# Down products of four blocks as seven-product quads, and gate/up quads that gather in three PSUM banks

## The chip, the cores and the metric

The kernel runs on one core of one Trainium2 chip. The metric is the time on the device, in microseconds (us). The engines are TensorE (PE), which multiplies; VectorE (DVE), ScalarE (ACT) and GpSimd (POOL), which work on tiles in SBUF and PSUM; and SyncE (SP), from whose queue nearly all DMAs are issued.

## The reference

One inference step of a backbone of two layers over 640 tokens (512 latent tokens and 128 context tokens) of 1024 channels. Each layer is a SwiGLU, a mixer, and a second SwiGLU, each behind an RMS norm with adaLN scale and shift, and each added to the residual stream x by a gate:

```
def swiglu(h, w_gate, w_up, w_down):
    return (jax.nn.silu(h @ w_gate) * (h @ w_up)) @ w_down

x = x + 0.5 * mod[:, 2][:, None, :] * swiglu(hh, ffn1_gate[l], ffn1_up[l], ffn1_down[l])
x = x + mod[:, 5][:, None, :] * y                 # y: the mixer's output
x = x + 0.5 * mod[:, 8][:, None, :] * swiglu(hh, ffn2_gate[l], ffn2_up[l], ffn2_down[l])
```

The inner width of a SwiGLU is 2816. The mixer of layer 0 is attention beside a gated linear recurrence, that of layer 1 a Fourier transform with a linear map. The change touches the four SwiGLUs alone.

## The kernel before

**Tiles.** Channels lie on the 128 partitions: 1024 channels are 8 chunks, the inner width is 22 chunks, called f. The tokens are held as two halves h = 0 and 1 of 320 columns each. The residual stream x stays in SBUF (`x_85` and `x_86` in the listings).

**Products.** Every product runs in fp32r as three passes, high × high, high × low and low × high (`mm3`, matmul at L282). So every weight and every right factor is split: ACT copies the high part (L176 for weights, `whi`; L171 for others), and DVE subtracts it from the value for the low part (L181, `wlo`; L172). Weights arrive by DMA in `st` buffers of 128 × 1024 (six in a SwiGLU), and their split parts take one of five slots; a quad's factor S1 has a slot of 512 columns of its own.

**Gate and up (`quad`).** For a chunk f from 2 on, the gate and up weights times the two token halves are a 2 × 2 problem (unit by half of the channels, half of the channels by half of the tokens). It takes seven products of 12 matmuls by Strassen and Winograd, 84 in place of 96:

M1 = A11 B11, M2 = A12 B21, M3 = S4 B22, M4 = A22 T4, M5 = S1 T1, M6 = S2 T2, M7 = S3 T3.

The right factors (B, T) come from the normed input and are made once for a SwiGLU. The left factors are made for each chunk by six steps (L214 to L249): a splits A11 and A12 as one part of 1024 columns; b and c make the sums S1, S3, S2 and S4 in four POOL operations of 512 columns (L226, L227, L231, L232; S1 into the one buffer `sums`); d splits S1 (`s`); e splits S3 beside A22, f splits S2 beside S4. The products run in the order M1, M5, M7, M6, M2, M3, M4, each in a PSUM bank of its own out of six; ACT copies M1, M5 and M7 to SBUF (L826), and DVE and POOL sum (L825). The result g of each half is then split (L171, L172).

**Down.** The 22 chunks go in blocks (`BLK`): six of three f and one of four. A block's down product takes each of the 8 output chunks and both token halves in a plain product over the block's f, 9 matmuls for three f (`down`), and DVE adds gate times the result to x straight from PSUM (`x_update`, L381; half 1 in pieces of 192 and 128 columns, since its tokens have two conditions). The last block (`down_last`) is interleaved with the next norm. A block's down product follows the quad of the next block's first chunk.

**Order.** The order on each engine is that of the program. `prep` emits weight steps from one list, one after each product, up to four items ahead, when its buffers are free; a low part is emitted with the step after its high part (`split_later`, `flush`). Fills (`fill`) are slabs of adaLN products between quads; the last SwiGLU has none there.

## Time and profile before

| | |
|---|---|
| Median of 3 runs | 2306.37 us (2303.54 to 2308.12) |
| Span of the profiled execution | 2305.0 us |
| PE busy | 2224.0 us, 96% |
| DVE busy | 1554.8 us, 67% |
| ACT busy | 990.7 us, 43% |
| POOL busy | 954.9 us, 41% |
| Granted TensorE clock | 0.992 |
| Instructions | 39901 |

The span is the time from the first to the last instruction of one profiled execution, which has no separate time of its own; the median is of other executions. Rows of the trace give an instruction's line, its engine, and `out<-in` by the program's names without buffer numbers. A row of a timeline has the start, the length, and in brackets the idle time before it with what ended it. A PE row of 0.31 us is the length of one matmul in the pipeline, and the next one begins before it ends; the time that a matmul takes up is the step from one start to the next.

### The profile page before, as it was taken

The numbers are of one execution on the slowest core, as the hardware profiler recorded it, in microseconds if no ns is written. First come the engines' busy times: TensorE is split into PE (matmuls) and PEld (weight loads), VectorE is DVE, ScalarE is ACT, GpSimd is POOL, SyncE is SP. The second block draws the span as 40 slices with busy tenths as digits, with TensorE's granted clock in tenths as the row PEclk, the third lists the DMA queues.
The fourth block names the chain that finished last, engine by engine and source line by source line (L and its number), as shares of the span: only waits on it lengthen the run. The fifth ranks groups of instructions, "written<-read, shape, count | busy, mean of one in ns | idle before, by whom it ended". The sixth has DMA issues, their size and how long they took to land.

```text
span 2305.0 us, 39901 instructions
## 1 busy us (share of the span) xinstructions
PE 2224.0 (96%) x15534; PEld 2110.0 (92%) x15534; DVE 1554.8 (67%) x2871; ACT 990.7 (43%) x1780; POOL 954.9 (41%) x856
## 2 busy tenths in 40 slices
PE   7999999999998899999999999999999989999999
PEld 5889999999994788999999889999999979999999
DVE  6676677666865368666666786666667786666665
ACT  4433333347855435333333453333335553333332
POOL 2444444440023235444444454444443645444441
PEclk9999999999999999999999999999999999999999
DMA  7333333321228424333322243332332322222221
GB/s 278 113 111 105 105 107 107 115 74 56 73 71 267 131 83 137 110 101 110 106 91 97 75 155 120 110 97 96 103 117 62 128 85 83 83 83 83 83 89 57
DMA packets 75316, 245.44 MB, mean 106 GB/s; under 512 B 8756, under 2 KB 12996, under 8 KB 75128
## 3 DMA queue, kind: packets, MB, share of 16 engines
q1 hardware_dynamic: 74168, 241.28, 31.7%
q8 instruction: 123, 2.02, 0.4%
q10 hardware_dynamic: 864, 1.38, 0.2%
q14 instruction: 65, 0.53, 0.1%
q0 software_dynamic: 96, 0.22, 0.0%
HBM read 239.71 MB, written 3.15 MB: 105 GB/s over the span
## 4 chain that ended last, share of the span: by engine, by line
PE 79%; DVE 13%; ACT 4%; issue 2%; POOL 2%; DMA 1%; ACTq 0%; DVEq 0%; SPq 0%; POOLq 0%
PE q L282 40%; PE pd L282 26%; PE pj L282 5%; DVE wlo L181 2%; PE ada L327 2%; DVE tl L172 1%; PE pg L282 1%; PE gt L1014 1%; PE pos L1549 1%; DVE x L381 1%; PE S L1262 1%; DVE y L473 1%; DVE sx L1268 1%; PE PT L1288 1%; DMA st<-w_ada 1%
## 5 line engine op out<-in xcount | busy, mean ns | idle before, releaser
L181 DVE TENSOR_TENSOR wlo<-st,whi 128x1024 fp32r<-128x1024 f32 (+2 forms) x401 | 498.4, 1254 | 11.1 <-ACT whi L176 10.2
L176 ACT ACTIVATE whi<-st 128x1024 fp32r<-128x1024 f32 (+2 forms) x405 | 401.2, 992 | 233.0 <-POOL st L232 139.3
L282 PE MATMUL pd<-g,whi 128*128 128x320 f32 x1536 | 347.0, 310 | 4.3 <-DVE u L825 2.3
L381 DVE SCALAR_TENSOR_TENSOR x<-pd,mods,x 128x128 f32<-128x128 f32 (+2 forms) x696 | 265.0, 433 | 111.7 <-PE pd L282 111.2
L282 PE MATMUL q<-hh,wlo 128*128 128x320 f32 x960 | 296.9, 309 | 5.3 <-DVE wlo L181 5.3
L282 PE MATMUL q<-hh,whi 128*128 128x320 f32 x960 | 300.7, 313 | 1.0 <-DVE u L825 1.0
L282 PE MATMUL q<-th,whi 128*128 128x320 f32 x960 | 297.3, 310 | 3.0 <-DVE sg L825 3.0
L282 PE MATMUL q<-tl,whi 128*128 128x320 f32 x960 | 296.6, 309 | 0.7 <-POOL tl L172 0.7
L282 PE MATMUL q<-th,wlo 128*128 128x320 f32 x960 | 296.6, 309 | 0.0
L282 PE MATMUL q<-hl,whi 128*128 128x320 f32 x960 | 296.3, 309 | 0.0
L231 POOL TENSOR_TENSOR st<-sums,st 128x512 f32<-128x512 f32 x80 | 118.0, 1474 | 396.9 <-DVE wlo L181 359.5
L825 POOL TENSOR_TENSOR u<-u,u 128x320 f32<-128x320 f32 x80 | 106.5, 1331 | 401.0 <-DVE u L825 401.0
L282 PEld LDWEIGHTS pd<-g,whi 128*128 128x128 f32 x1536 | 256.8, 188 | 8.9 <-DVE x L381 3.1
L282 PE MATMUL pd<-hh,whi 128*128 128x320 f32 x768 | 238.4, 310 | 0.0
L282 PE MATMUL pd<-hl,whi 128*128 128x320 f32 x768 | 237.9, 310 | 0.0
L282 PE MATMUL pd<-g,wlo 128*128 128x320 f32 x768 | 237.7, 310 | 0.0
L282 PE MATMUL pd<-hh,wlo 128*128 128x320 f32 x768 | 236.8, 308 | 0.0
L826 ACT ACTIVATE sg<-sg 128x320 f32<-128x320 f32 x160 | 75.4, 471 | 284.5 <-DVE sg L825 284.5
L282 PEld LDWEIGHTS q<-hh,whi 128*128 128x128 f32 x960 | 180.2, 188 | 16.8 <-issue 8.6
L282 PEld LDWEIGHTS q<-th,whi 128*128 128x128 f32 x960 | 180.3, 188 | 6.6 <-issue 4.7
L282 PEld LDWEIGHTS q<-hh,wlo 128*128 128x128 f32 x960 | 180.2, 188 | 6.4 <-DVE wlo L181 6.4
L282 PEld LDWEIGHTS q<-tl,whi 128*128 128x128 f32 x960 | 180.4, 188 | 1.5 <-POOL tl L172 1.5
(327 smaller groups left out, 5016.0 us busy)
## 6 DMA issues: line engine op xcount, KB each, us to landing
st<-w_ada SPq DMA_DIRECT2D x144, 512.0 KB, 4.6
st<-ffn_gate SPq DMA_DIRECT2D x88, 512.0 KB, 3.6
st<-ffn_up SPq DMA_DIRECT2D x88, 512.0 KB, 3.7
st<-ffn_down SPq DMA_DIRECT2D x96, 384.0 KB, 3.1
st<-w_in SPq DMA_DIRECT2D x20, 512.0 KB, 3.5
st<-ffn_down SPq DMA_DIRECT2D x16, 512.0 KB, 3.5
st<-w_out_ab SPq DMA_DIRECT2D x8, 512.0 KB, 3.5
st<-w_out_c SPq DMA_DIRECT2D x8, 512.0 KB, 3.5
```

Source lines behind the costliest of these rows:

```text
L172: (eng or self.nc.vector).tensor_tensor(out=lo, in0=src, in1=hi.bitcast(F32), op=ALU.subtract)
L176: self.nc.scalar.activation(out=hi, in_=src, func=AF.Copy)
L181: self.low.tensor_tensor(out=lo, in0=src, in1=hi.bitcast(F32), op=ALU.subtract)
L231: self.nc.gpsimd.tensor_tensor(out=s[:, 0:512], in0=it.s1, in1=s[:, 0:512], op=ALU.subtract)
L282: self.nc.tensor.matmul(out, lhsT=l, rhs=r, start=first and j == 0, stop=last and j == len(ops) - 1)
L327: nc.tensor.matmul(self.ada_ps[32 * j:32 * j + 32, 0:256], lhsT=self.s_sb[:, k, :], rhs=t[:, 256 * j:256 * j + 256], start=k == 0, stop=k ...
L381: self.nc.vector.scalar_tensor_tensor(out=self.x[h][c][:, sl], in0=ps[:, sl], scalar=gate[:, c, r:r + 1], in1=self.x[h][c][:, sl], op0=ALU ...
L473: nc.vector.tensor_tensor(out=y, in0=self.x[h][c], in1=r, op=ALU.mult)
L825: tt = lambda e, o, a, b, op=ALU.add: e.tensor_tensor(out=o, in0=a, in1=b, op=op)
L826: cp = lambda o, p, fn=AF.Copy: nc.scalar.activation(out=o, in_=p, func=fn)
L1014: nc.tensor.matmul(g[:, s, 0:322], lhsT=wt[:, d, j, :], rhs=xc[:, 322 * s:322 * s + 322], start=True, stop=True)
L1262: nc.tensor.matmul(o, lhsT=q, rhs=k, start=True, stop=True)
```

## The change

In each SwiGLU the blocks become four of four f, one of two and one of four. In the first four blocks the down product is done by `down_quad`, twice for a block, once for each four output chunks. It is again a 2 × 2 problem: two output chunks by two f-chunks on the left, two f-chunks by two token halves on the right, for two pairs of outputs q and two pairs of f at once. Each of the seven products is 12 matmuls (two banks q, two pairs of f, three passes), so a down quad has 84 where the plain form has 96, and a block 168 where it has 192. The last six f keep plain products.

The right factors are now made of g. `g_even` and `g_odd` make them for a pair of f (B11, T1; B22, B21, T3, T2, T4), with high parts on ACT (L744 of the changed kernel), low parts on DVE (L747) and subtractions on POOL (L758); `step` advances each by one stage after every product. The result of the last quad before a down product is held back (`g_held`) and goes into its factors only after the two down quads.

A gate/up quad's products run in a new order and gather in three banks: a takes A11, then S2, S1 and S4 on top; b takes S3, then A22; c takes A12. Between them ACT copies the bank to SBUF (L1022): m1, g1 (from b), g0, u5. A product that adds to a bank waits until ACT has copied the sum so far. The steps of the weights are a, b, c, e, f, d. A down quad does the same with pairs of banks (copies at L939), and adds to x in twelve updates of 320 columns, six of which read the copies instead of PSUM (L388); the plain form has eight, all from PSUM.

Also changed: the tags `u3` and `c22` have three buffers each; the heads of the SwiGLUs finish the T factors earlier (`t_end` at (6, 1, 1) instead of (6, 3, 1)); two small parameter loads are issued from ACT's queue instead of POOL's, and the scratch for dynamic DMA is 1024; the down weights are laid out to suit.

```diff
-BLK = (3,) * 6 + (4,)
+BLK = (4,) * 4 + (2, 4)
+NS = 4
...
+GN = ("B11", "B21", "B22", "T1", "T2", "T3", "T4")
+PLAIN = {16: (0, ("B11", "T1")), 17: (0, ("B21", "B22")), 18: (0, ("T2", "T3")), 19: (1, ("B11", "B21")),
+         20: (0, ("B11", "T1")), 21: (0, ("B21", "B22"))}
...
-        s = [(self.quad_a, 1), (self.quad_b, 0), (self.quad_c, 0), (self.quad_d, 2), (self.quad_e, 1), (self.quad_f, 1)]
+        s = [(self.quad_a, 1), (self.quad_b, 0), (self.quad_c, 0), (self.quad_e, 1), (self.quad_f, 1), (self.quad_d, 2)]
         if first:
-            s = s[:3] + s[5:] + s[3:5]
+            s = s[:3] + [s[4], s[5], s[3]]
...
-            w = 2 * nb * P
-            for c in range(0, KD, 2):
-                self.add_w(dn[off:off + P * w].rearrange("(p w) -> p w", p=P), w, ph)
+            w = 1024 if bi < NS else 2 * nb * P
+            part = lambda: dn[off:off + P * w].rearrange("(p w) -> p w", p=P)
+            for c in range(4):
+                if bi < NS and c % 2:
+                    self.add_quad(a0, part(), ph, False)
+                elif bi < NS:
+                    a0 = part()
+                else:
+                    self.add_w(part(), w, ph)
                 off += P * w
...
+    def g_even(self, G, b11, b12):
+        self.hi(G["B11"], b11)
+        yield 1
+        self.lo(G["B11"], b11)
+        yield 1
+        self.sub(b11, b12, b11)
+        yield 1
+        self.hi(G["T1"], b11)
+        yield 1
+        self.lo(G["T1"], b11)
+    def g_odd(self, G, t1, b12, b21, b22):
+        self.hi(G["B22"], b22)
+        self.sub(b12, b22, b12)
+        yield 1
+        self.hi(G["B21"], b21)
+        self.lo(G["B22"], b22)
+        self.sub(t1, b22, t1)
+        yield 1
+        self.lo(G["B21"], b21)
+        self.hi(G["T3"], b12)
+        yield 1
+        self.hi(G["T2"], t1)
+        self.lo(G["T3"], b12)
+        self.sub(b21, b21, t1)
+        yield 1
+        self.lo(G["T2"], t1)
+        self.hi(G["T4"], b21)
+        yield 1
+        self.lo(G["T4"], b21)
...
+    def g_put(self, f, g0, g1, wait=False):
+        if wait:
+            self.g_held = f, g0, g1
+        elif f >= 4 * NS:
+            self.g_jobs.append(self.g_plain(f, g0, g1))
+        elif f % 2 == 0:
+            self.g_last = g0, g1
+            self.g_jobs.append(self.g_even(self.G[f // 2 % 2], g0, g1))
+        else:
+            self.g_jobs.append(self.g_odd(self.G[f // 2 % 2], *self.g_last, g0, g1))
...
-                self.quad(f, qfills.pop(0))
+                self.quad(f, qfills.pop(0), wait=bi < NS and f == end - 1)
                 next(mid, None)
                 f += 1
             if bi == 0:
                 self.ada_end()
             fs = range(sum(BLK[:bi]), sum(BLK[:bi + 1]))
-            if bi == len(BLK) - 1:
+            self.g_end()
+            if bi < NS:
+                for d in range(2):
+                    self.down_quad(d, gate)
+                self.g_put(*self.g_held)
+            elif bi == len(BLK) - 1:
...
+        def mm(p, name, x, first=True, last=False, free=None):
+            for q in pq:
+                self.mm3(p[q], self.need(it, name), (2 * q, 2 * q + 1), [G[x] for G in self.G], first, last, True)
+            if free == "S1":
+                self.s1_free.append(it.slot.pop("S1"))
+            elif free:
+                self.free_slot(it, free)
+        def snap(p, *tags):
+            ts = [self.temp(tags[q % len(tags)]) for q in pq]
+            for t, b in zip(ts, p):
+                nc.scalar.activation(out=t, in_=b, func=AF.Copy)
+            return ts
+        def add(h, i, v):
+            for q in pq:
+                self.x_update(h, 4 * d + 2 * q + i, v[q], gate)
+        a = bank()
+        mm(a, "A11", "B11")
+        m1 = snap(a, "acc0", "acc1")
+        self.step()
+        b = bank()
+        mm(b, "S3", "T3")
+        m7 = snap(b, "c22")
+        self.step()
+        mm(a, "S2", "T2", False)
+        u2 = snap(a, "u3")
+        self.step()
+        c = bank()
+        mm(c, "A12", "B21", last=True, free="A1")
+        add(0, 0, c)
+        self.step()
+        mm(a, "S1", "T1", False, free="S1")
+        u5 = snap(a, "sq")
+        for q in pq:
+            nc.gpsimd.tensor_tensor(out=m7[q], in0=m7[q], in1=u5[q], op=ALU.add)
+        add(0, 0, m1)
+        self.step()
+        mm(b, "A22", "T4", False, True, "S3")
+        add(0, 1, b)
+        self.step()
+        mm(a, "S4", "B22", False, True, "S24")
+        add(1, 0, a)
+        self.step()
+        add(0, 1, u2)
+        add(1, 1, m7)
+    def temp(self, tag):
+        bufs = {"acc0": 1, "acc1": 1, "sq": 2}.get(tag)
+        if bufs:
+            return self.t2.tile([P, HT], F32, tag=tag, name="tmp", bufs=bufs)
+        return self.t3.tile([P, HT], F32, tag=tag, name=f"t{tag}", bufs=3)
+    def step(self):
+        self.prep(self.n_use + 4, 1)
+        self.g_step()
...
+        if chain:
+            it = self.item()
+            a = mm("A11", None, False)
+            m1 = snap(a, "acc0")
+            step()
+            b = mm("S3", None, False)
+            g1 = snap(b, "c22")
+            step()
+            mm("S2", a, False)
+            g0 = snap(a, "u3")
+            step()
+            self.fill(fills // 2)
+            c = mm("A12")
+            sg0, sg1 = sgs()
+            tt(nc.vector, sg0, c, m1)
+            step()
+            mm("S1", a, False)
+            u5 = snap(a, "sq")
+            act(sg0, sg0, AF.Silu)
+            tt(nc.gpsimd, g1, g1, u5)
+            step()
+            mm("A22", b)
+            tt(nc.vector, g0, b, g0)
+            tt(nc.vector, g0, g0, sg0, ALU.mult)
+            step()
+            mm("S4", a)
+            act(sg1, a, AF.Silu)
+            self.ada_end()
+            step()
+            tt(nc.vector, g1, g1, sg1, ALU.mult)
```

The first place is a gate/up quad that follows one of odd f, on ACT, in the last SwiGLU. Before, a quad's row of ACT has its copies of M1 (`m_20481`), M5 (`m_20498`) and M7 (`u_20499`), the high parts of weights (`whi`, `s`) and the two SiLUs.

```order
L826 ACTIVATE m_20481<-q 128x320
L826 ACTIVATE m_20498<-q 128x320
L176 ACTIVATE s_18906<-sums 128x512
L826 ACTIVATE u_20499<-q 128x320
L176 ACTIVATE whi_73<-st_18904 128x1024
L826 ACTIVATE sg<-sg 128x320
L176 ACTIVATE whi_75<-st_18905 128x1024
L826 ACTIVATE sg<-sg 128x320
L171 ACTIVATE g_18910<-c_20501 128x320
```

After, at the end of quad 7 and the start of quad 8: the copies are m1 (`tmp`), g1 (`tc_20490`) and g0 (`tu_20508`), and between them stand high parts of right factors (L744; `hh_91` is that of T3, from `tc_20234`).

```order
L183 ACTIVATE s_18990<-sums 128x512
L183 ACTIVATE whi_73<-st_66 128x1024
L1022 ACTIVATE sg<-q 128x320
L744 ACTIVATE g1B_19010<-tc_20363 128x320
L1022 ACTIVATE tmp<-q 128x320
L183 ACTIVATE whi_67<-st_64 128x1024
L744 ACTIVATE g1B_19008<-tu_20380 128x320
L1022 ACTIVATE tc_20490<-q 128x320
L744 ACTIVATE hh_91<-tc_20234 128x320
L1022 ACTIVATE tu_20508<-q 128x320
L744 ACTIVATE hh_89<-tu_20252 128x320
```

The high part of T3 now stands ahead of the copy of g0, for which the quad's S1 product waits.

On POOL, in a quad before, the four sums of the next weight split are followed by the three sums of the quad's results.

```order
L226 TENSOR_TENSOR sums<-st_18903 128x512
L227 TENSOR_TENSOR st_18903<-st_64,st_18903 128x512
L231 TENSOR_TENSOR st_64<-sums,st_64 128x512
L232 TENSOR_TENSOR st_64<-st_64 128x512
L825 TENSOR_TENSOR u_22855<-u_22855,u_22856 128x320
L825 TENSOR_TENSOR u_22856<-u_22856,m_22854 128x320
L825 TENSOR_TENSOR c_22857<-u_22855,m_22854 128x320
```

After, at the same place as on ACT above, one sum of results (L1021) of quad 7 comes first, then the four sums of the split, then three subtractions (L758), of which the first makes T3 (`tc_20234`).

```order
L1021 TENSOR_TENSOR tc_20363<-tc_20363,tmp 128x320
L233 TENSOR_TENSOR sums<-st_64 128x512
L234 TENSOR_TENSOR st_64<-st_66,st_64 128x512
L238 TENSOR_TENSOR st_66<-sums,st_66 128x512
L239 TENSOR_TENSOR st_66<-st_66 128x512
L758 TENSOR_TENSOR tc_20234<-tc_20363,tc_20234 128x320
L758 TENSOR_TENSOR tu_20252<-tc_20363,tu_20252 128x320
L758 TENSOR_TENSOR tu_20380<-tu_20380,tu_20252 128x320
L1021 TENSOR_TENSOR tc_20490<-tc_20490,tmp 128x320
```

T3 is made behind the four sums of the split, and the first of these writes `sums`, which DVE's low part of quad 7's S1 reads.

The other place is a down product, on DVE. Before, the updates of x (`x_85` half 0, `x_86` half 1) read PSUM (`pd`) and stand between low parts of weights.

```order
L181 TENSOR_TENSOR wlo_76<-st_64,whi_75 128x768
L381 SCALAR_TENSOR_TENSOR x_85<-pd,mods,x_85 128x320
L381 SCALAR_TENSOR_TENSOR x_86<-pd,mods,x_86 128x192
L381 SCALAR_TENSOR_TENSOR x_86<-pd,mods,x_86 128x128
L381 SCALAR_TENSOR_TENSOR x_85<-pd,mods,x_85 128x320
L381 SCALAR_TENSOR_TENSOR x_86<-pd,mods,x_86 128x192
L381 SCALAR_TENSOR_TENSOR x_86<-pd,mods,x_86 128x128
L181 TENSOR_TENSOR wlo_74<-st_18904,whi_73 128x1024
L181 TENSOR_TENSOR s_18907<-sums,s_18906 128x512
```

After, at the end of the first down quad of a block: four updates from PSUM, a low part, then six updates that read the copies u2 (`tu`) and m7 (`tc`).

```order
L388 SCALAR_TENSOR_TENSOR x_86<-pd,mods,x_86 128x192
L388 SCALAR_TENSOR_TENSOR x_86<-pd,mods,x_86 128x128
L388 SCALAR_TENSOR_TENSOR x_86<-pd,mods,x_86 128x192
L388 SCALAR_TENSOR_TENSOR x_86<-pd,mods,x_86 128x128
L188 TENSOR_TENSOR wlo_68<-st_18989,whi_67 128x1024
L388 SCALAR_TENSOR_TENSOR x_85<-tu_20639,mods,x_85 128x320
L388 SCALAR_TENSOR_TENSOR x_85<-tu_20640,mods,x_85 128x320
L388 SCALAR_TENSOR_TENSOR x_86<-tc_20621,mods,x_86 128x192
L388 SCALAR_TENSOR_TENSOR x_86<-tc_20621,mods,x_86 128x128
L388 SCALAR_TENSOR_TENSOR x_86<-tc_20622,mods,x_86 128x192
L388 SCALAR_TENSOR_TENSOR x_86<-tc_20622,mods,x_86 128x128
```

The updates from m7 now come last, and they free the `c22` buffers into which ACT copies the next quad's product S3.

More of the change, by code (lines that the diff above doesn't have):

```diff
@@ L273, in done, with mm3 @@
         self.prep(self.n_use + self.LS, most)
-    def mm3(self, out, w, ks, xs, first=True, last=True):
+    def mm3(self, out, w, ks, xs, first=True, last=True, skip=False):
         ops = []
@@ L715, in gpart, with g_step, g_end, hi @@
     def gpart(self, f, h):
-        return self.g[f % 4][2 * h:2 * h + 2]
-    def g_split(self, f, h, gg):
-        self.split(*self.gpart(f, h), gg)
+        k, n = PLAIN[f]
+        return self.G[k][n[h]]
+    def g_step(self):
+        self.g_jobs = [g for g in self.g_jobs if next(g, None)]
+    def g_end(self):
+        while self.g_jobs:
+            self.g_step()
+    def hi(self, t, src):
+        self.nc.scalar.activation(out=t[0], in_=src, func=AF.Copy)
+    def lo(self, t, src):
+        self.nc.vector.tensor_tensor(out=t[1], in0=src, in1=t[0].bitcast(F32), op=ALU.subtract)
@@ new lines, in g_plain, with sub @@
+    def g_plain(self, f, g0, g1):
+        two = [(self.gpart(f, h), g) for h, g in enumerate((g0, g1))]
+        for t, g in two:
+            self.hi(t, g)
+        yield 1
+        for t, g in two:
+            self.lo(t, g)
+    def sub(self, o, a, b):
+        self.nc.gpsimd.tensor_tensor(out=o, in0=a, in1=b, op=ALU.subtract)
+    def g_even(self, G, b11, b12):
[8 more added lines that the diff above has]
+        self.lo(G["T1"], b11)
@@ L790, in ffn_body, with down_quad @@
                     self.done()
+    def down_quad(self, d, gate):
+        nc = self.nc
+        it = self.item()
+        pq = range(2)
+        bank = lambda: [self.bank("pd")[:, 0:HT] for _ in pq]
+        def mm(p, name, x, first=True, last=False, free=None):
[49 more added lines that the diff above has]
+        self.prep(self.n_use + 4, 1)
+        self.g_step()
     def down(self, p, w, j, h, fs, now):
@@ L818, in down_last, with quad, mm @@
                 self.done()
-    def quad(self, f, fills, begin=False):
+    def quad(self, f, fills, begin=False, wait=False):
         nc = self.nc
         tt = lambda e, o, a, b, op=ALU.add: e.tensor_tensor(out=o, in0=a, in1=b, op=op)
-        cp = lambda o, p, fn=AF.Copy: nc.scalar.activation(out=o, in_=p, func=fn)
-        t3 = lambda n, bufs=2: self.t3.tile([P, HT], F32, tag=n, name=n, bufs=bufs)
+        act = lambda o, p, fn=AF.Copy: nc.scalar.activation(out=o, in_=p, func=fn)
         h, T = self.h, self.T
-        step = lambda: self.prep(self.n_use + 4, 1)
-        def mm(name, xs, free=None):
-            p = self.bank("q")[:, 0:HT]
-            self.mm3(p, self.need(it, name), range(4), xs)
+        step = self.step
+        XS = {"A11": h[0][:4], "A12": h[0][4:], "S4": h[1][4:], "A22": T[3], "S1": T[0], "S2": T[1], "S3": T[2]}
+        chain = f > 2
+        SLOT = {"A12": "A1", "S4" if chain else "S2": "S24", "A22": "S3", "S1": "S1"}
+        def mm(name, p=None, last=True):
+            first = p is None
+            if first:
+                p = self.bank("q")[:, 0:HT]
+            self.mm3(p, self.need(it, name), range(4), XS[name], first, last, chain)
+            free = SLOT.get(name)
             if free == "S1":
@@ L885, in quad, with snap @@
-        tt(nc.vector, u3, u3, sg0, ALU.mult)
-        self.g_split(f, 0, u3)
+        def snap(p, tag):
+            t = self.temp(tag)
+            act(t, p)
+            return t
+        sgs = lambda: [self.t2.tile([P, HT], F32, tag="y", name="sg", bufs=3) for _ in range(2)]
+        if chain:
+            it = self.item()
+            a = mm("A11", None, False)
[26 more added lines that the diff above has]
+            tt(nc.vector, g1, g1, sg1, ALU.mult)
+        else:
+            if not self.begun:
+                it = self.item()
+                m1 = snap(mm("A11"), "acc0")
+                step()
+                c = None
+            else:
+                it, m1, c = self.begun
+            if begin:
+                self.begun = it, m1, mm("A12")
+                return
+            if c is None:
+                c = mm("A12")
+                step()
+            e = mm("S4")
+            step()
+            m5 = snap(mm("S1"), "sq")
+            step()
+            g0 = snap(mm("S3"), "u3")
+            step()
+            self.fill(fills // 2)
+            u2 = self.temp("sq")
+            g1 = self.temp("c22")
+            tt(nc.vector, u2, mm("S2"), m1)
+            tt(nc.gpsimd, g0, g0, u2)
+            tt(nc.gpsimd, u2, u2, m5)
+            tt(nc.gpsimd, g1, g0, m5)
+            step()
+            sg0, sg1 = sgs()
+            tt(nc.vector, sg0, c, m1)
+            act(sg0, sg0, AF.Silu)
+            step()
+            tt(nc.vector, sg1, e, u2)
+            act(sg1, sg1, AF.Silu)
+            tt(nc.vector, g1, g1, sg1, ALU.mult)
+            step()
+            tt(nc.vector, g0, mm("A22"), g0)
+            self.ada_end()
+            tt(nc.vector, g0, g0, sg0, ALU.mult)
@@ L887, in quad @@
+        self.g_put(f, g0, g1, wait)
         step()
```

117 lines of the change are left out of this document (61 added, 56 removed).

## The prediction

> **What bounds the kernel now.** I read the page's head, then the granted clock, then the chain that ended last, then a table by stage, the waits and the timelines. The head shows a TensorE (PE) that is busy almost throughout, and the clock is nearly full, so it is not the throttle that sets the time.
>
> ```profile
> span 2305.0 us, 39901 instructions
> PE 2224.0 (96%) x15534; PEld 2110.0 (92%) x15534; DVE 1554.8 (67%) x2871; ACT 990.7 (43%) x1780; POOL 954.9 (41%) x856
> core 0: 2305.0 us, clock 0.992
> ```
>
> The profiled span of 2305.0 us lies 1.4 below the median of 2306.37, so sums made in the trace carry over to the median as they are. The chain (start, length, what, count) is PE from product to product. Its rows from the last SwiGLU are three gate/up quads (252 matmuls), one down block (144), and three quads; the rows of an earlier one show quads with one fill (an adaLN slab, 8 narrow matmuls) between.
>
> ```profile
> 1473.07 0.57 PE ada L327 x8
> 1473.64 12.52 PE q L282 x84
> ...
> 1945.59 36.98 PE q L282 x252
> 1982.56 21.13 PE pd L282 x144
> 2003.69 36.96 PE q L282 x252
> ```
>
> Hence 21.13/144 = 0.1467 us for a matmul of 320 columns, 1.76 us for a product of twelve, 12.32 us for a quad of 84, and 0.57 for a fill. The table by stage (window, length, then busy time and count of PE, PEld, DVE, ACT, POOL, then clock, DMA share, GB/s) says that PE never stops in the steady state, while the others have room; the waits there (total, times, longest) are on the side of those others.
>
> ```profile
> 1945.00:2275.00 330.00, 330.00 (x2251) 330.00 (x2251) 214.96 (x354) 129.88 (x216) 149.32 (x120) 1.00 0.24 77
> POOL st L231 <- DVE wlo L181: 88.9, 17, 8.4
> ACT whi L176 <- POOL st L232: 28.5, 11, 5.4
> ```
>
> So taking matmuls away shortens the time, as long as the steps that feed PE keep up. Whether they do is the question, and the timelines of DVE and POOL give the prices (start, length, instruction):
>
> ```profile
> 2021.04 1.22 DVE L181 TENSOR_TENSOR wlo<-st,whi 128x1024 fp32r<-128x1024 f32 x1
> 2022.17 0.68 DVE L181 TENSOR_TENSOR s<-sums,s 128x512 fp32r<-128x512 f32 x1
> 2023.50 1.58 DVE L181 TENSOR_TENSOR wlo<-st,whi 128x1024 fp32r<-128x1024 f32 x1
> 2022.42 1.58 POOL L231 TENSOR_TENSOR st<-sums,st 128x512 f32<-128x512 f32 x1 [4.75 <-DVE wlo L181]
> 2024.08 2.16 POOL L232 TENSOR_TENSOR st<-st 128x512 f32<-128x512 f32 x1
> 2026.20 0.87 POOL L825 TENSOR_TENSOR u<-u,u 128x320 f32<-128x320 f32 x1
> ```
>
> The low part that starts at 2023.50 ends at 2025.08, 1.07 after POOL's first sum ended at 2024.00; POOL's second ends at 2026.24, 1.16 after that. They run one after the other: each holds the other off for its whole length. The holds are so 1.07 us for a low part of 1024 columns and 1.16 for a POOL sum of 512. A lone instruction reads 0.15 longer (1.22 against 1.07), so by the rows I take 0.53 for s, 0.73 for a POOL sum of 320, and 0.35 for a DVE operation of 320 that reads two SBUF tiles (0.49 lone). Where DVE reads PSUM and SBUF, there is no such hold: four updates take 0.41 each beside two POOL sums at their lone length.
>
> ```profile
> 2059.40 1.65 DVE L381 SCALAR_TENSOR_TENSOR x<-pd,mods,x 128x320 f32<-128x320 f32 x4
> 2059.63 1.29 POOL L231 TENSOR_TENSOR st<-sums,st 128x512 f32<-128x512 f32 x1 [3.19 <-DVE wlo L181]
> 2061.00 1.30 POOL L232 TENSOR_TENSOR st<-st 128x512 f32<-128x512 f32 x1
> ```
>
> **What is removed.** In each of four SwiGLUs, four blocks of four f-chunks go from 192 to 2 × 84 = 168 matmuls, 24 fewer each: 16 × 24 = 384, which is also the difference of the two programs' PE rows. All were on the chain: 384 × 0.1467 = **−56.3 us**. The last six f-chunks of a SwiGLU keep plain down products.
>
> **What is added and moved.** Per block, two weight splits with four POOL sums, three low parts and s, in place of four plain low parts; right factors of g (7 high parts on ACT, 7 low parts on DVE, 4 POOL subtractions for a pair of f); and, of twelve updates of x in a down quad, six that read SBUF copies instead of PSUM. In holds, a split is 4 × 1.16 + 3 × 1.07 + 0.53 = 8.38, six of them 50.3; the four gate/up quads add 4 × (0.73 + 2 × 0.35) = 5.7; the two pairs' factors 2 × (4 × 0.73 + 7 × 0.35) = 10.7; the down quads 2 × (2 × 0.73 + 6 × 0.35) = 7.1. That is 73.8 us in a block in which PE has 504 × 0.1467 = 73.9, or 76.2 with four fills. DVE and POOL together are thus as full as PE, and any place where one waits in order for the other shows on PE. Two families of places do, by the order of instructions.
>
> *B: the gate/up quad after one of odd f (quads 4, 6, 8, … 16 of a SwiGLU, 28 in all).* S1 is now its fifth product, into a bank that ACT must first have copied out (the copy of g0). On ACT, the high part of T3 stands ahead of that copy; T3 is a POOL subtraction queued behind the four sums of the next weight split; the first of these waits for DVE's low part of S1 (one sums buffer), and that stands behind the previous quad's last two operations on g0. Durations of ACT and the delay from PE to DVE come from these rows (groups: busy, mean ns; the matmul that closes a product issues at 2010.42, the slot after it ends at 2010.57, and DVE starts at 2010.76):
>
> ```profile
> L171 ACT ACTIVATE hh<-u 128x320 fp32r<-128x320 f32 x40 | 18.9, 472 | 76.6 <-DVE u L825 76.6
> L826 ACT ACTIVATE m<-q 128x320 f32<-128x320 f32 x160 | 63.2, 429 | 177.5 <-PE q L282 177.5
> L176 ACT ACTIVATE whi<-st 128x1024 fp32r<-128x1024 f32 x300 | 315.3, 1053 | 227.0 <-POOL st L232 139.3 <-PE pd L282 71.8 <-PE yp L1588 6.2
> 2010.42 0.31 PE L282 MATMUL q<-th,wlo 128*128 128x320 f32 x1
> 2010.76 0.49 DVE L825 TENSOR_TENSOR u<-q,m 128x320 f32<-128x320 f32 x1 [1.84 <-PE q L282]
> ```
>
> From the end of A22: 0.19 + two operations on g0 0.82 + s 0.6 + four sums 4.64 + T3 0.73 + its high part 0.5 + the copy 0.5 = 8.0. Five products pass meanwhile (S4, A11, S3, S2, A12): 8.8. So it is hidden if nothing of DVE's falls between. But two low parts of 1024 and three operations of 320 stand there (2.14 + 1.05 = 3.2), and each takes its turn with a POOL sum: 11.2, a wait of 2.4. I take 2.0, since one of the short ones may miss; a fill before it gives 0.57 back, and all but the last SwiGLU have it: 7 × 2.0 + 21 × 1.4 = **+43 us** (ends 0 and 7 × 2.4 + 21 × 1.8 = 55).
>
> *C: the quads behind a down quad.* A down quad's last updates (m7, tag c22) free the buffers into which the next quad copies S3; that copy stands on ACT ahead of a weight's high part and of the copies that S1 waits for. From the end of the first down quad: 0.19, four updates from PSUM 1.45, a low part 1.07, two updates from u2 0.7, the pieces of m7 0.7, and, if these take turns with POOL, three sums of 512 3.48; then ACT's copy 0.43, high part 1.05, two copies 0.86: 9.9, of which the first sum partly runs beside the updates from PSUM, so about 9.0. S1 is wanted after four products, at 7.04. The wait is 1.3 to 1.95 in the second down quad (I take 1.5), and 1.0 to 1.5 in the gate/up quad after it, which needs only one buffer (1.2). 16 × 1.5 + 16 × 1.2 = **+43 us** (ends 0 and 55). Without turns the chain is 9.9 − 3.5 = 6.4 and nothing shows. Which of the two holds rests on whether an update with two SBUF operands behaves like the L381 rows or like the low parts. The nearest row is the same instruction with both operands in SBUF (min/median/max ns), and its maximum is a stretch of 0.8 us, as a hold would make:
>
> ```profile
> L492 DVE SCALAR_TENSOR_TENSOR hl<-y,mods,hh x20: 541/574/1351, 32.2 to 1861.0; 128x320 fp32r<-128x320 f32 x20
> ```
>
> So I take the holds. The Trainium skill, page "SBUF — State Buffer", section "Who interferes with whom", says that a DVE instruction with two SBUF inputs and a GpSimd instruction that reads SBUF exclude each other, and that one with at most one SBUF input does not contend; the L181/L231 and L381 rows agree with both halves. By that rule the moved updates contend and C is paid; without it the sum is that of the second rival.
>
> *Edits with small prices.* Banks, 3 instead of 6 for a gate/up quad: the copies that free them are C's and B's own. The heads' earlier T steps and the early waits of the plain f-chunks: +3, with ±5 as bounds, since PE idles only 81 us (2305.0 − 2224.0) in the whole span and a few us of these lie there. DMAs from ACT's queue at the start (two issues): at most some tenths, as the first product waits for x and weights.
>
> Sum: 2306.4 − 56.3 + 43 + 43 + 3 = **2339 us**.
>
> **The rivals.** *R1, all is hidden (faster).* DVE and POOL run ahead far enough that neither chain starts late. For it: POOL waits 88.9 of 330 us and ACT 28.5 in the steady state, so there is slack; against it: the holds fill 73.8 of 73.9 to 76.2 us, and B starts from A22, which no running ahead moves. It gives 2306.4 − 56.3 + 3 = 2253, and 2274 where a quarter of the 86 us shows. *R2, one family only.* If updates from SBUF pass POOL freely, C goes and 2339 − 43 = 2296 remains; if the short steps miss B's chain, the same. For it: C's ends reach zero; against it: the L492 row. *R3, the pair DVE and POOL is the bound everywhere (slower still).* It decides once turns are packed below 91%: at 88% a block takes 73.8/0.88 = 83.9 in place of 528 × 0.1467 = 77.5, or 79.8 in the twelve blocks with fills: 12 × 4.1 + 4 × 6.4 = +75, 2381. For it: 73.8 against 73.9; against it: these engines' turns overlap by the 0.15 at each end, and PE's waits at B and C give them time. That the change does not do what it says can be excluded for the matmuls, which are 384 fewer in the program.
>
> **How the numbers follow.** Forecast (both families; its own range is 2318 to 2360, with the 86 us a quarter smaller or larger): 0.50. R1: 0.18. R2: 0.12. A remainder of about 53 of the 86 us, which is a tie: 0.08. R3: 0.12. A measurement of this kernel can tell 0.2%, 4.6 us, from no change. Faster is R1 and R2, 0.30; same 0.08; slower is the forecast and R3, 0.62. The range goes from 2268, which leaves out about 0.11 of R1, to 2380, which leaves out some 0.07 of R3.
>
> **What would show it.** In the changed kernel's trace, right are: 12,768 matmuls of L289; PE waits for ACT at S1 of quads 4, 6, 8 … of 1 to 2.4 us, and at S1 of the second down quad and of the quad after it; updates from tmp, tu and tc that stretch to 1 us or more beside POOL. Wrong: a chain that is still PE without waits at these places (R1); waits in one kind only (R2); PE waits spread over many products with DVE or POOL busy without gaps (R3). A span below 2285 would refute the size of both families.

## The result, and the profile after

The changed kernel takes 2481.98 us (median of 4 runs, 2481.19 to 2484.02) against 2306.64 us before: a ratio of 1.0758, with a 95% interval of 1.0742 to 1.0773. The forecast was 2339 us, so the direction was right and the size was not: 175 us slower instead of 33. The profiled execution has a span of 2479.3 us, 174.3 more than that of the kernel before. The page's head shows first where that lies.

```profile
span 2479.3 us, 39704 instructions
PE 2233.9 (90%) x15150; PEld 2101.2 (85%) x15150; DVE 1869.7 (75%) x2895; ACT 1201.1 (48%) x2256; POOL 1305.6 (53%) x1030
```

The granted clock of the core:

```profile
core 0: 2479.3 us, clock 0.964
```

PE's busy time rose by 9.9 us although 384 matmuls (56.3 us) are gone: its other matmuls took 66.2 us longer, and the granted clock fell from 0.992 to 0.964. PE's idle time rose from 81.0 to 245.4 us, by 164.4. So 164.4 + 66.2 − 56.3 = 174.3. The waits of PE (total, times, longest) name the idle time; the kernel before had 14 us of waits at q and pd in all.

```profile
PE q L289 <- ACT tu L1022: 75.6, 43, 3.0
PE q L289 <- ACT tmp L1022: 48.9, 17, 10.1
PE pd L289 <- ACT tu L939: 38.8, 16, 3.9
PE q L289 <- DVE wlo L188: 16.7, 3, 5.6
```

By their place in the program, 27 of the 43 waits in the first row are the forecast's B (42.1 us) and 16 are C's in the quad after a down quad (33.5 us); the third row is C in the second down quad. The other two rows are mostly the heads of the SwiGLUs: four waits of 8.2 to 10.1 us in quad 3 (36.9 us) and three of 5.6 us in quad 2. The table by stage over the last SwiGLU's steady part says the same (before: PE 330.00 of 330.00 at a clock of 1.00):

```profile
2055.00:2410.00 355.00, 320.11 (x2061) 314.48 (x2060) 276.17 (x363) 168.04 (x308) 219.91 (x152) 0.96 0.24 73
```

One wait of the B family, in the chain that ended last (start, length, what): four POOL sums, T3's subtraction, ACT's high part of T3, ACT's copy, and only then PE. It is the row of steps of the forecast, one by one.

```profile
1055.52 2.19 POOL sums L233
...
1057.79 1.44 POOL st L234
...
1059.30 1.44 POOL st L238
...
1060.80 2.16 POOL st L239
1062.96 1.07 POOL tc L758
...
1064.05 0.47 ACT hh L744
1064.52 0.33 ACT tu L1022
...
1064.90 5.11 PE q L289 x33
```

The C family, at the end of a first down quad: DVE's two updates from the copies u2 take 3.07 us, because each takes a turn with a POOL sum, and the copy that PE waits for comes after m7's pieces (timelines of DVE, POOL and ACT).

```profile
2089.03 3.07 DVE L388 SCALAR_TENSOR_TENSOR x<-tu,mods,x 128x320 f32<-128x320 f32 x2
2092.03 2.29 DVE L388 SCALAR_TENSOR_TENSOR x<-tc,mods,x 128x192 f32<-128x192 f32 x4
2088.11 2.15 POOL L234 TENSOR_TENSOR st<-st,st 128x512 f32<-128x512 f32 x1
2090.34 1.42 POOL L238 TENSOR_TENSOR st<-sums,st 128x512 f32<-128x512 f32 x1
2091.84 1.42 POOL L239 TENSOR_TENSOR st<-st 128x512 f32<-128x512 f32 x1
2093.85 0.44 ACT L939 ACTIVATE tc<-pd 128x320 f32<-128x320 f32 x1 [4.46 <-DVE x L388]
```

The groups by tile (min/median/max ns) show the price of a turn: the update that always meets POOL takes 1.57 us, and the same instruction from the copy m1, which mostly does not, 0.54. (POOL's rows in these traces have operands in SBUF alone; what POOL sums out of PSUM, ACT copies to SBUF first.)

```profile
L388 DVE SCALAR_TENSOR_TENSOR x<-tu,mods,x x64: 1568/1576/1629, 160.5 to 2370.2; 128x320 f32<-128x320 f32 x64
L388 DVE SCALAR_TENSOR_TENSOR x<-tmp,mods,x x64: 539/544/1180, 153.2 to 2361.8; 128x320 f32<-128x320 f32 x64
```

The heads, which the forecast had not seen: in quad 3 of the last SwiGLU, ACT reaches the copy of A11's product at 2047.15, eleven microseconds after the product was through. Two high parts stand ahead of it, and the first, that of the right factor T4, waits 5.41 us for POOL. S2, which adds to that bank, waits for the copy.

```profile
2046.42 0.47 ACT L744 ACTIVATE g0T<-t 128x320 fp32r<-128x320 f32 x1 [5.41 <-POOL t L797]
2046.79 0.45 ACT L744 ACTIVATE g1B<-tu 128x320 fp32r<-128x320 f32 x1
2047.15 0.42 ACT L1022 ACTIVATE tmp<-q 128x320 f32<-128x320 f32 x1
2047.62 0.64 PE L289 MATMUL q<-th,whi 128*128 128x320 f32 x1 [9.78 <-ACT tmp L1022]
```

The slow matmuls: here are two B waits of nearly the same length.

```profile
2067.68 0.42 PE L289 MATMUL q<-th,s 128*128 128x320 f32 x1 [2.15 <-ACT tu L1022]
2157.59 0.41 PE L289 MATMUL q<-th,s 128*128 128x320 f32 x1 [2.14 <-ACT tu L1022]
```

In the 4 us behind the first the clock was 0.57 and 17 matmul records began, behind the second 1.00 and 27:

```profile
2067.70:2071.70 4.00, 4.00 (x17) 4.00 (x18) 2.97 (x5) 2.54 (x6) 1.29 (x2) 0.57 0.07 19
2157.60:2161.60 4.00, 4.00 (x27) 4.00 (x28) 3.19 (x6) 3.40 (x7) 2.23 (x2) 1.00 0.11 11
```

### The profile page after: what moved, and what is told of

Same layout as the page of the kernel before. It is cut to its first block, busy times and chain, and to the rows that moved or that the text cites. A ratio compares the mean times of both kernels' runs of the same rounds, so it can differ in the third digit from the quotient of the medians.

```text
span 2479.3 us, 39704 instructions
## 1 busy us (share of the span) xinstructions
PE 2233.9 (90%) x15150; PEld 2101.2 (85%) x15150; DVE 1869.7 (75%) x2895; ACT 1201.1 (48%) x2256; POOL 1305.6 (53%) x1030
## 4 chain that ended last, share of the span: by engine, by line
PE 45%; DVE 25%; POOL 16%; issue 8%; ACT 5%; DMA 2%; SPq 0%; ACTq 0%; POOLq 0%; DVEq 0%
PE q L289 19%; PE pd L289 14%; DVE x L388 10%; DVE wlo L188 5%; PE pj L289 5%; POOL sums L233 3%; POOL st L239 3%; POOL st L234 2%; POOL st L238 2%; ACT whi L183 1%; DVE tl L179 1%; PE pg L289 1%; PE ada L334 1%; POOL tc L758 1%; POOL tu L758 1%
## 5 line engine op out<-in xcount | busy, mean ns | idle before, releaser
L188 DVE TENSOR_TENSOR wlo<-st,whi 128x1024 fp32r<-128x1024 f32 (+1 forms) x417 | 552.0, 1325 | 112.2 <-ACT whi L183 109.4
L183 ACT ACTIVATE whi<-st 128x1024 fp32r<-128x1024 f32 (+1 forms) x421 | 434.2, 1033 | 200.4 <-POOL st L234 71.2
L233 POOL TENSOR_TENSOR sums<-st 128x512 f32<-128x512 f32 x112 | 206.4, 1843 | 207.1 <-DVE s L188 157.7
L289 PE MATMUL q<-hh,wlo 128*128 128x320 f32 x960 | 299.1, 312 | 16.7 <-DVE wlo L188 16.7
L388 DVE SCALAR_TENSOR_TENSOR x<-pd,mods,x 128x320 f32<-128x320 f32 (+2 forms) x472 | 191.5, 447 | 101.5 <-PE pd L289 100.8
L289 PE MATMUL q<-th,s 128*128 128x320 f32 x640 | 168.1, 332 | 75.6 <-ACT tu L1022 75.6
L1021 POOL TENSOR_TENSOR tc<-tc,tmp 128x320 f32<-128x320 f32 x76 | 85.8, 1129 | 265.5 <-ACT tmp L1022 265.5
L239 POOL TENSOR_TENSOR st<-st 128x512 f32<-128x512 f32 x112 | 190.1, 1698 | 8.8
L234 POOL TENSOR_TENSOR st<-st,st 128x512 f32<-128x512 f32 x112 | 188.0, 1679 | 8.8
L289 PEld LDWEIGHTS q<-th,wlo 128*128 128x128 f32 x960 | 186.5, 194 | 0.0
L289 PEld LDWEIGHTS q<-hl,whi 128*128 128x128 f32 x960 | 182.0, 190 | 0.0
L289 PE MATMUL pd<-g0B,whi 128*128 128x320 f32 x768 | 175.3, 311 | 0.0
```

The source lines that it names most:

```text
L183: self.nc.scalar.activation(out=hi, in_=src, func=AF.Copy)
L188: self.low.tensor_tensor(out=lo, in0=src, in1=hi.bitcast(F32), op=ALU.subtract)
L233: self.nc.gpsimd.tensor_tensor(out=it.s1, in0=u1[:, 0:512], in1=u1[:, 512:], op=ALU.add)
L234: self.nc.gpsimd.tensor_tensor(out=u1[:, 0:512], in0=u0, in1=u1[:, 0:512], op=ALU.subtract)
L239: self.nc.gpsimd.tensor_tensor(out=s[:, 512:], in0=s[:, 512:], in1=s[:, 0:512], op=ALU.subtract)
L289: self.nc.tensor.matmul(out, lhsT=l, rhs=r, start=first and j == 0, stop=last and j == len(ops) - 1, skip_group_check=skip)
```

## The experiments

Two theories stood after the result. *Order*: each wait comes from what stands ahead in ACT's and POOL's queues, and goes when that is moved. *Full pair* (the forecast's R3): DVE and POOL, which hold each other off, have no time left, and the places of the waits are only where that shows. Each time is a median; the ratio is to the kernel before, measured beside it (2306.2 to 2306.9 us).

**e1, factors first.**

```diff
     def step(self):
-        self.prep(self.n_use + 4, 1)
         self.g_step()
+        self.prep(self.n_use + 4, 1)
```

> The changed kernel with one edit: in step, the right factors' stage is issued ahead of the weight step, so POOL subtracts T3 two sums earlier and, of ACT's copies in a quad after an odd f, none waits for the fourth sum. Order theory (each wait of PE comes from what stands ahead in ACT's and POOL's queues, and goes with it): the 27 waits of the B family (46 us in the trace of the changed kernel, and 13 us of slowly clocked matmuls behind them) go; about 2422 us. Rival, full-pair theory (DVE and POOL, which hold each other off, have no time left, so a wait that is removed comes back elsewhere): less than 30 us gained, above 2452.

Measured: 2459.39 us, 1.0662 (1.0645 to 1.068), 22.6 less than the change. All 27 waits of B are gone; the 16 left in the second row are C's. But the waits for `tmp` went from 48.9 to 78.2 us: S4 now waits for the copy u5, which stands behind a right factor's high part that POOL delivers late, and behind a weight's. The time lies in the full pair's range (above 2452) and far from order's 2422: order decides the place, and in place of B's 42.1 us, 32.8 us of waits came up at S4 of the same quads.

```profile
PE q L289 <- ACT tmp L1022: 78.2, 45, 8.3
PE q L289 <- ACT tu L1022: 25.7, 16, 3.1
```

**e2, five buffers for c22; e3, T factors late; e4, the three together.** (e2: `bufs=5` in place of 3 for that tag; e3 in the heads:)

```diff
-                    if (n, j, h) == (6, 1, 1):
+                    if (n, j, h) == (6, 3, 1):
```

> The changed kernel with one edit: five buffers instead of three for tag c22, so that the copy of S3 need not wait for the last updates of x of the down quad before. Order theory: the C waits (41 us in the second down quads, 36 us in the quads after them, and 34 us of slow matmuls behind them) go; about 2371 us. Full-pair theory: the updates and sums still take turns, and the waits move to other places; less than 55 us gained, above 2426.

> The changed kernel with one edit: the T factors end at (6, 3, 1) in the heads as in the kernel before. Order theory: the three waits of 5.7 us for DVE's low part at the first quad shrink to the 1.8 us of the kernel before, with a microsecond of slow matmuls each; about 2467 us, and the waits of 8 to 10 us in quad 3 stay. If the T factors' place doesn't matter: within 4 us of the changed kernel.

> The three edits together. Order theory: the gains add up, 60 + 111 + 15 = 186; about 2296 us, slightly under the kernel before. Full-pair theory: above 2390, with PE's waits spread over other places and DVE or POOL without gaps there.

Measured: e2 2419.63 us, 1.0489 (1.0473 to 1.0506), 62 less, between the two forecasts (2371, and above 2426). The waits in the second down quads are gone and 2.5 us are left of the 33.5 behind them, so the missing buffer was their cause; but `tmp` rose to 70.4 us. e3: 2480.51 us, 1.5 less, where order had said 2467; quad 2's waits for DVE's low part fell from 16.7 to 2.5 us, and those of quad 3 at S2 grew from 36.9 to 48.3, the longest to 13.4 us. e4: 2402.63 us, 1.0414 (1.0397 to 1.0431), where order had said 2296 and the full pair over 2390. Of B and C one wait of 0.5 us is left, and `tmp` has 56 waits with 116.7 us. Mending the order brings 79 of the 186 us that order had added up for those places.

**e5 to e7, more order.** e5 gives `sums` a second buffer (and c22 four), e6 issues no weight step between A12 and S1, e7 puts the head's six factor sums on DVE.

```diff
-        return self.t2.tile([P, 512], F32, tag="sums", name="sums", bufs=1)
+        return self.t2.tile([P, 512], F32, tag="sums", name="sums", bufs=2)
...
             tt(nc.vector, sg0, c, m1)
-            step()
+            self.g_step()
             mm("S1", a, False)
```

> Factors first (as in e1), four buffers for c22 and two buffers for sums (five and two don't fit together). POOL's first sum of a weight split no longer waits for DVE's low part of the previous S1. Chain theory (what is late is POOL's row of sums and subtractions, which starts at that low part): the waits of 1.1 to 1.7 us that e1 showed at S4 shrink to under half; the heads' waits of 7 to 11 us stay; about 2365 us. Full-pair theory: above 2390.

> As e5, and no weight step is issued between A12 and S1 of a gate/up quad, so that the high part of S2 and S4 stands behind ACT's copy u5 instead of ahead of it. Chain theory: of the waits left at S4 those that end with that high part go; 5 to 15 us under e5. Full-pair theory: within 4 us of e5.

> As e6, and the six sums that make the right factors of the first two f-chunks run on DVE instead of POOL. If the heads' wait of 7 to 11 us in quad 3 comes from POOL's row of sums (ACT's high part of T4 stands ahead of the copy m1): it falls under 4 us in each SwiGLU, some 25 to 38 us in all with the slow matmuls behind it. If DVE is as full there as POOL: within 5 us of e6.

Measured: 2409.84, 2423.40 and 2426.14 us. In e5 the waits at S4 of the quads after one of odd f did shrink (24 waits with 11.3 us, 32.8 us in e1), but 24 others with 23.9 us came up at S2; it has 71 waits for `tmp` in all with 83.7 us, and with four c22 buffers 26.8 us stayed in the second down quads: no gain over e4's 2402.63. In e6 the later step cost 14 us, which neither theory had forecast. In e7 the longest wait of the heads was 10.1 us against 10.8 in e6, although its sums had moved from POOL to DVE. All three times missed what the order theory had expected; those of e5 and e7 lie in the ranges of its rival.

**e8 and e9, less for the pair to do.** e8 is e7 with the two sums of step c on DVE; e9 is that edit alone, on the change as it is.

```diff
     def quad_c(self, it, w):
         s = it.raw[0][0]
-        self.nc.gpsimd.tensor_tensor(out=s[:, 0:512], in0=it.s1, in1=s[:, 0:512], op=ALU.subtract)
-        self.nc.gpsimd.tensor_tensor(out=s[:, 512:], in0=s[:, 512:], in1=s[:, 0:512], op=ALU.subtract)
+        self.nc.vector.tensor_tensor(out=s[:, 0:512], in0=it.s1, in1=s[:, 0:512], op=ALU.subtract)
+        self.nc.vector.tensor_tensor(out=s[:, 512:], in0=s[:, 512:], in1=s[:, 0:512], op=ALU.subtract)
```

> As e7, and the two sums of weight step c run on DVE, where one takes 0.53 us of the shared turn instead of 1.16: 6 x 2 x 0.63 = 7.6 us less in a block of some 76. Both theories: faster than e7. Full-pair theory: by most of 16 x 7.6 = 120 us as far as waits are left. Chain theory: by the waits of PE that end with POOL, at least 20 us; about 2300 us in all.

> The changed kernel with one edit: the two sums of weight step c run on DVE instead of POOL. Full-pair theory (PE waits because DVE and POOL together have no time left; the places of the waits are only where that shows): the pair has 7.6 us less to do in a block of some 80, and the waits of all families shrink, C's too, with the slow matmuls behind them; about 2385 us. Order theory: only B's chain, which holds these sums, gets shorter, by 1.3 us in 27 places, and C's waits for the c22 buffers stay over 2 us; about 2440 us.

Measured: e8 2340.09 us, 1.0146 (1.0129 to 1.0163), 86 less than e7; e9 2353.38 us, 1.0201 (1.0184 to 1.0218), 129 us less than the change by two lines, more than the three order edits together. Nothing about the c22 buffers was touched, and yet C's waits fell from 38.8 and 33.5 us to 9.3 and 14.3. The sum takes 0.69 us on DVE where it took 1.42 on POOL, and in the last SwiGLU PE is back at a clock of 1.00 and 316.44 of 330 us. Of the two forecasts the full pair's (2385) is the nearer one, and e9 went beyond both.

But e9 doesn't decide between them, since the two moved sums stand in both chains themselves. In B's chain above they are the L238 and L239 ahead of T3, 1.44 and 2.16 us. In C's place the updates took turns with them; in e9 DVE does them behind the updates, which end sooner (3.07 and 2.29 us in the change):

```profile
1995.48 2.04 DVE L388 SCALAR_TENSOR_TENSOR x<-tu,mods,x 128x320 f32<-128x320 f32 x2
1997.45 1.26 DVE L388 SCALAR_TENSOR_TENSOR x<-tc,mods,x 128x192 f32<-128x192 f32 x4
```

That is 2.1 us off C's chain, about as much as a typical C wait, and order's forecast had left it out. What is left is mostly the heads, in the first two rows. The waits of e9:

```profile
PE q L289 <- ACT tmp L1022: 50.6, 23, 11.6
PE q L289 <- DVE wlo L188: 16.5, 3, 5.6
PE q L289 <- ACT tu L1022: 14.3, 16, 1.0
...
PE pd L289 <- ACT tu L939: 9.3, 7, 1.6
```

Its first sum of step c, now on DVE (min/median/max ns):

```profile
L238 DVE TENSOR_TENSOR st<-sums,st x112: 674/692/1362, 77.7 to 2300.4; 128x512 f32<-128x512 f32 x112
```

Its steady part of the last SwiGLU:

```profile
1960.00:2290.00 330.00, 316.44 (x2113) 310.61 (x2113) 292.73 (x418) 169.79 (x313) 154.30 (x107) 1.00 0.26 80
```

And the same sum in the changed kernel, on POOL:

```profile
L238 POOL TENSOR_TENSOR st<-sums,st x112: 1259/1417/1442, 77.8 to 2426.4; 128x512 f32<-128x512 f32 x112
```

**e10 to e12, the heads.** e10 gives quad 3 a bank for each product and ends the T factors late; e11 adds to that factors first, five c22 buffers and step c on DVE; e12 is e11 with two buffers for sums and four for c22.

```diff
-        chain = f > 2
+        chain = f > 3
...
-                self.add_quad(gt[f], up[f], ph, f == 2)
+                self.add_quad(gt[f], up[f], ph, f < 4)
```

> The changed kernel with the heads as before: quad 3 takes the form with a bank for each product (as quad 2 has), and the T factors end at (6, 3, 1). If the heads' waits (55 us and 14 us of slow matmuls) come from the three banks, which let PE run ahead of ACT and DVE by one product instead of five while these catch up: they fall to a quarter, about 2430 us. If what DVE and POOL are behind by the head shows later all the same, in quads 4 and 5: within 15 us of the changed kernel.

> Factors first, five buffers for c22, step c on DVE, quad 3 unchained and the T factors late. If the causes found are the whole: e8's 2340 less 50 for the heads and 17 for its waits in the second down quads; about 2275 us, 1.3% under the kernel before. If the heads can't be mended: about 2325.

> As e11 with two buffers for sums and four for c22. Waits for a c22 buffer of a microsecond stay in the second down quads, as in e8; 5 to 15 us above e11.

Measured: 2479.62, 2343.35 (1.0162, 1.0147 to 1.0177) and 2343.63 us. The second theory of e10 holds: the long waits broke up into shorter ones in quads 3 and 4 (up to 6.0 us), and the time stayed. One quad with more banks was not enough for what ACT and DVE are behind by. e11 is above both of its forecasts (2275 and 2325), and e12 is level with it, where 5 to 15 us more were expected.

**e13, the gather alone.** All blocks get plain down products (no right factors of g); the gate/up quads gather in three banks.

```diff
+QB = ()
...
-            w = 1024 if bi < NS else 2 * nb * P
+            w = 1024 if bi in QB else 2 * nb * P
```

> The changed kernel without its down quads: all blocks (four, four, four, four, two, four) have plain down products, the gate/up quads gather in three banks as in the change. Full-pair theory: a block of four f now holds the pair for 4 x 8.38 + 4 x 1.07 + 5.7 + 8 x 0.35 = 46 us of 77.5, and the B and C waits are gone. For the heads: if their 55 us come from the right factors of the first f-chunks, these are gone too, and the time is that of the kernel before, within 10 us; if they come from the three banks, they stay: 2306 + 50 to 65, about 2360 us.

Measured: 2364.11 us, 1.0249 (1.0234 to 1.0264). B and C are gone, and the heads stay: 23.2 us in quad 3 and 20.1 us at DVE's low parts, more than four fifths of its 51 us of waits at q. So the right factors make the smaller part of the heads' waits: without them those of quad 3 fell from 36.9 to 23.2 us. e13 alone doesn't show that the rest is the gather's, since it keeps the T factors early and the change's other small edits; e17 below is the other side of that.

```profile
PE q L290 <- ACT tmp L1027: 28.7, 13, 6.9
PE q L290 <- DVE wlo L189: 20.1, 4, 6.6
```

**e14 to e16, a plain first block.** `QB = (1, 2, 3)`: on e9 (e14), on e11 (e15), and on e15 with quad 3 and the T factors as in the change (e16).

> As e9 (step c on DVE), and the first block of each SwiGLU has a plain down product, so that no right factors are made in the head; that adds 4 x 24 matmuls, 14 us. If the heads' waits (51 us and 17 us of slow matmuls in e9) come from the right factors: about 2353 + 14 - 50 = 2317 us. If from the three banks: about 2365 us.

> As e11, and the first block of each SwiGLU has a plain down product. e11 has 85 us of waits at q and 34 us of slow matmuls, nearly half of them in the heads. If the right factors of the head are what DVE and POOL are behind with there: 2343 + 14 - 60, about 2297 us, under the kernel before. If not: about 2357 us.

> Factors first, five c22 buffers, step c on DVE, plain first block; quad 3 gathers in three banks and the T factors end early, as in the change. Against e15 it shows what the heads' form is worth once no right factors are made there: 10 to 40 us above e15 if PE's running ahead matters then, within 5 us if not.

Measured: 2354.19, 2339.78 (1.014, 1.0125 to 1.0156) and 2346.57 us. With 14 us of matmuls added, e14 stands level with e9: the right factors of the head cost about 13 us, not 50. e15 lies between its two forecasts (2297 and 2357), and e16 is 6.8 us above e15, between its two. e15 is with e8 the fastest version of the change, and still 1.4% behind the kernel before.

**e17 and e18, the down quads alone.** All gate/up quads have a bank for each product, as before the change; e17 is otherwise the change with the T factors late, e18 is e11.

```diff
-        chain = f > 2
+        chain = f > 99
```

> The other part of the change alone: down quads as in the change, all gate/up quads with a bank for each product and the T factors late, as in the kernel before. The heads' waits should fall to those of the kernel before (some 5 us each instead of 14), which is 40 to 60 us with the slow matmuls; the B waits lose their cause (no copy of a partial sum), but POOL has two more sums of 0.73 us in a quad, 5.8 us in a block. If waits follow order: about 2482 - 55 - 60, about 2370 us. If they follow the pair's load (73.8 + 5.8 = 79.6 in a block whose PE has 76): what B loses appears elsewhere, above 2420.

> As e11 (factors first, five c22 buffers, step c on DVE, T factors late), but all gate/up quads with a bank for each product. The pair's load is 73.8 + 5.8 - 7.6 = 72 us of 76 in a block. If the three banks are what ties PE to the engines that lag in the heads and at S4: e11's 2343 less most of its 85 us of waits and 34 us of slow matmuls, about 2275 us, under the kernel before. If a load of 72 of 76 is still too much: 2320 or more.

Measured: 2629.20 us, 1.1394 (1.1375 to 1.1413), and 2538.74 us, 1.1009 (1.0993 to 1.1025). Both are far above what order had forecast (2370 and 2275). They lie in the open ranges of the full pair (above 2420, and 2320 or more), but not in the order of its loads: e18 gives the pair 72 us of work in a block where the change gives it 73.8, and takes 57 us longer. So the pair's load alone does not set the time. The old quad has two more POOL sums; that is 93 us of holds in the 16 blocks, and e17 lies 147 us above the change. In both kernels the largest wait stands at the first down quad of a block, 16 times about 5 us. In e18:

```profile
PE pd L289 <- ACT tmp L939: 90.7, 16, 5.7
PE q L289 <- DVE tu L1021: 27.2, 19, 2.8
```

There ACT's copies of the first product stand behind a SiLU of the quad before and behind a weight's high part, which wait for DVE and POOL:

```profile
2305.19 0.47 ACT L1022 ACTIVATE sg<-sg 128x320 f32<-128x320 f32 x1 [2.53 <-DVE sg L1021]
2308.11 1.06 ACT L183 ACTIVATE whi<-st 128x1024 fp32r<-128x1024 f32 x1 [2.45 <-POOL st L234]
2309.07 0.75 ACT L939 ACTIVATE tmp<-pd 128x320 f32<-128x320 f32 x2
```

In the heads (quads 2 to 4 of the four SwiGLUs) PE waits 31.4 us in all in e17, the longest 4.9 us, against 63.4 in the change, 46.4 in e13 and 10.0 in the kernel before. In e3, from which e17 differs by the gather alone, they are 63.9. So the gather doubles the heads' waits when the down quads are there, and brings more of them than the down quads do.

So the change in its two parts:

| | plain down products | down quads |
|---|---|---|
| a bank for each product | 2306.6 (before) | 2629.2 (e17) |
| gather in three banks | 2364.1 (e13) | 2482.0 (the change) |

The down quads alone cost 323 us, the gather alone 57, both together 175. With down quads the gather gains 147 us; without them it loses 57. How much of the 147 comes from the two POOL sums that it takes out of each quad, and how much from where ACT's copies stand (e18's rows above), no run tells apart. (The kernel before has blocks of three f and none of the change's small edits, and e17 ends the T factors late, which by e3 is worth 1.5 us.)

## Why the prediction was wrong, point by point

- *Removed, −56.3 us*: right. The matmuls are 384 fewer, and the time of one at full clock is what it was.
- *B, +43 us*: right in place, mechanism and size: 42.1 us. The typical wait was 1.6 us behind a fill and 2.1 without, where the forecast took 1.4 and 2.0. The chain of waits above is the forecast's chain. Part of the agreement is luck: in the first SwiGLU the waits were only 0.4 to 1.2 us, and one of the 28 places had none.
- *C, +43 us*: right in place and mechanism, too small: 72.3 us. The forecast's chain summed to 9.9 us, of which it kept 9.0 for an overlap; it took waits of 1.5 and 1.2 us, inside ends that reached 55 in all. In the trace each update takes a full turn (1.57 us), and the waits were 2.0 to 3.9 in the second down quad and up to 3.0 behind it. That updates from SBUF take turns with POOL is shown.
- *"The heads' earlier T steps ... +3, with ±5 as bounds, since PE idles only 81 us"*: the first step that failed. It priced an edit by the idle time of a kernel that did not have it. The heads, with short waits elsewhere, cost about 51 us more than before (53.6 us in seven waits and 12 us of short ones, less the 14 of the kernel before). Three of the seven (16.7 us) stand in quad 2, which has a bank for each product in both kernels; they come from the T factors' earlier place, and e3 mostly moved them into quad 3. *"Banks, 3 instead of 6 ...: the copies that free them are C's and B's own"* put the rest at nothing: quad 3's S2 waits 8.2 to 10.1 us for one copy of its own quad, and by e13 and e17 the gather brings the larger part of the heads' waits.
- *No term for the clock*: the second step that failed, and the larger one. That "it is not the throttle that sets the time" was read from a kernel whose PE hardly waits in the SwiGLUs, and each new wait was priced at its own length. The matmuls that are left took 66 us longer, most of it right behind the waits (last section).
- Together: −56.3 + 42.1 + 72.3 + 51 + 66 = 175, the measured difference within a microsecond.
- *R3, 12%, "the pair DVE and POOL is the bound everywhere", 2381*: argued, not shown, as the mechanism behind B and C. For it: what was mended at one copy came back in part at the next (e1, e4, e5), and two sums less for POOL brought 129 us (e9). Against it: the waits did not spread over many products, as its sign had said; e9 shortens both local chains as well; and e18, with less load than the change, is slower. What e1 and e4 do show is that B and C cannot be priced one by one and added up, as the forecast did.
- *R1 and R2* are out: B and C both showed in full.

What stays open is whether the pair's load or the order in ACT's and POOL's queues makes B and C as long as they are, and how much of the heads' 55 us belongs to the copies in quad 3 and how much to the T factors' place. e3 and e10 mostly shift the latter from one place to the other. Whether the gather could pay with the heads mended was not tried to the end; the down quads never came below 2339.8 us.

## What to carry to other kernels

Add up the times of two engines that hold each other off, stage by stage. When the sum comes near that of the bounding engine, do not price waits one by one: what is mended at one comes back in part at the next. The sum is a warning and not a forecast, as e18 shows. Here taking two sums off POOL, which DVE does in half the time, was worth more than three edits of order together. A scheme that saves on the bounding engine by giving it fewer buffers, or by making its products wait for copies, has to be judged where the other engines are furthest behind, which here was the heads and not the steady state. And a new wait of the bounding engine is priced with what its clock loses behind it.

## What the runs showed of the hardware that was not expected

A wait of PE costs more than its length. Behind the wait of 3.0 us that began at 2108.8 the matmuls of 320 columns started 0.267 us apart instead of 0.147, from 2112.5 to 2116:

```profile
2114.58 0.47 PE L289 MATMUL q<-th,whi 128*128 128x320 f32 x1
2114.85 0.47 PE L289 MATMUL q<-tl,whi 128*128 128x320 f32 x1
...
2116.53 0.31 PE L289 MATMUL q<-th,whi 128*128 128x320 f32 x1
2116.68 0.31 PE L289 MATMUL q<-tl,whi 128*128 128x320 f32 x1
```

That is 1.8 us lost on top of the 3.0. In the changed kernel's trace, waits up to 1.7 us cost 0.1 to 0.5 us more; waits of 2.0 to 2.5 us cost 0.1 or 1.4 to 1.8 us, the two windows above being one of each; waits from 3 us on cost 1.5 us or more. The Trainium skill, page "TensorE: Matmul & The Clock Gate", section "What's actually happening", says that PE's clock is halved after an idle window of about 3.4 us and back after a busy one, and that the window runs freely. The nearly doubled step, its length of some 3.5 us and the chance in it agree with the trace; but here idle times of 2.0 to 2.2 us were enough in some places (a clock of 0.57 behind the one of 2.15), and the measurement decides.
